# Instance norm in 3D on one core: three 64 KiB slots, each store one load behind, squares on two engines

## The chip, the cores and the metric

The kernel runs on one core of one Trainium2 chip. The metric is the device time of one execution, in microseconds (us); lower is better. The core has a matrix engine (PE), VectorE (DVE), ScalarE (ACT), GpSimd (POOL) and SyncE (SP), which run their own instruction streams and meet at semaphores. Data moves between the device memory (HBM) and the on-chip memory (SBUF, 128 partitions) by transfers that SP issues here; 16 DMA engines carry them out. PSUM is the small memory that PE writes its products to.

## What is computed

```python
# x: (8, 64, 32, 64, 64) float32, eps: 1e-5
mean = np.mean(x, axis=(2, 3, 4), keepdims=True)
var = np.var(x, axis=(2, 3, 4), keepdims=True)
return ((x - mean) / np.sqrt(var + eps)).astype(np.float32)
```

There are 8 x 64 = 512 instances of 32 x 64 x 64 = 131,072 numbers, 512 KiB each. Every number is read once and written once: 268.44 MB in and 268.44 MB out. The variance is taken in a second pass over the data in SBUF, around the mean that the first pass gave.

## The kernel before

**Tiling.** An instance is spread over 16 partitions (`SPLIT`), so a tile holds 8 instances: 128 partitions of 8192 columns, 32 KiB in each partition, 4 MiB in all. There are 64 tiles. The pool has six buffers (`SLOTS`).

**One tile's work** (`compute`, L80). `cut` is half of the columns. DVE sums the first half (L83) while ACT sums the second (L86, an Identity activation whose accumulator is the sum; its written output, `unused`, is thrown away). A matmul with a block matrix of 1/131,072 (L93) adds the sums of an instance's 16 partitions, so that each partition gets the two halves of its instance's mean, and DVE adds them with a minus sign (`neg_mean`, L95). ACT then squares the whole tile with that bias and accumulates (L103). A second matmul gives the variance (L107), ACT takes the square root (L109), DVE the reciprocal (`scale`, L111) and the product `bias` (L113). Then the tile is normalized in place: DVE the second half (L114), ACT the first (L122).

**Order.** Everything stands in the order written (`manual_schedule`). The loop (L130) first loads and computes tile g, then stores tile g - 4 (`LAG`). All loads (L77) and stores (L135) are issued by SP and go through one queue, in order. SP's stream is thus five loads, then a store and a load in turn, and five stores after the last load. A store waits on SP for both engines' last work on its tile. From the seventh on, a load waits on SP until the store that empties its buffer has landed; everything behind it in SP's stream waits too.

The lines that the change and the steps below touch are L77, L83, L86, L93, L95, L103, L107, L114, L122, L135 and the loop at L130.

Of the kernel before, what the change touches and what calls it, by code (L numbers as in the profile page):

```python
# [1 line left out]

# [4 lines left out]


@with_exitstack
def kernel(  # L10
    ctx: ExitStack,
    tc: tile.TileContext,
    x: bass.AP,
    eps: bass.AP,
    out: bass.AP,
):
    nc = tc.nc
    fp32 = mybir.dt.float32
    Alu = mybir.AluOpType
    Act = mybir.ActivationFunctionType  # L20

    P = 128
    B, C, D, H, W = x.shape
    n_inst = B * C
    n_elem = D * H * W
    eps_f = float(eps)

    SPLIT = 16
    IPT = P // SPLIT
    F = n_elem // SPLIT  # L30
    n_tiles = n_inst // IPT
    SLOTS = 6

    x_t = x.rearrange("b c d h w -> (b c) (d h w)").rearrange(
        "(k i) (s f) -> k (i s) f", i=IPT, s=SPLIT
    )
    out_t = out.rearrange("b c d h w -> (b c) (d h w)").rearrange(
        "(k i) (s f) -> k (i s) f", i=IPT, s=SPLIT
    )

    singles = ctx.enter_context(tc.tile_pool(name="singles", bufs=1))
    data_pool = ctx.enter_context(tc.tile_pool(name="data", bufs=SLOTS))
    stat_pool = ctx.enter_context(tc.tile_pool(name="stats", bufs=4))
    psum_pool = ctx.enter_context(
        tc.tile_pool(name="psum", bufs=2, space=bass.MemoryType.PSUM)
    )


    avg = singles.tile([P, P], fp32, name="avg")
    nc.vector.memset(avg, 1.0 / n_elem)  # L50
    nc.gpsimd.affine_select(  # L51
        out=avg,
        in_=avg,
        pattern=[[-SPLIT, IPT], [0, SPLIT]],
        compare_op=Alu.is_ge,
        fill=0.0,
        base=0,
        channel_multiplier=1,
    )
    nc.gpsimd.affine_select(  # L60
        out=avg,
        in_=avg,
        pattern=[[SPLIT, IPT], [0, SPLIT]],
        compare_op=Alu.is_ge,
        fill=0.0,
        base=SPLIT - 1,
        channel_multiplier=-1,
    )

    eps_t = singles.tile([P, 1], fp32, name="eps_t")  # L70
    nc.vector.memset(eps_t, eps_f)  # L71

    unused = singles.tile([P, F], mybir.dt.uint8, name="unused")

    def load(g):
        t = data_pool.tile([P, F], fp32, name="xt")
        nc.sync.dma_start(out=t, in_=x_t[g])  # L77
        return t

    def compute(t):  # L80
        cut = F // 2
        sums = stat_pool.tile([P, 2], fp32, name="sums")
        nc.vector.reduce_sum(  # L83
            out=sums[:, 0:1], in_=t[:, :cut], axis=mybir.AxisListType.X
        )
        nc.scalar.activation(  # L86
            out=unused[:, cut:],
            in_=t[:, cut:],
            func=Act.Identity,
            accum_out=sums[:, 1:2],  # L90
        )
        mean_ps = psum_pool.tile([P, 2], fp32, name="mean_ps")
        nc.tensor.matmul(out=mean_ps, lhsT=avg, rhs=sums, start=True, stop=True)  # L93
        neg_mean = stat_pool.tile([P, 1], fp32, name="neg_mean")
        nc.vector.tensor_reduce(  # L95
            out=neg_mean,
            in_=mean_ps,
            axis=mybir.AxisListType.X,
            op=Alu.add,
            negate=True,  # L100
        )
        squares = stat_pool.tile([P, 1], fp32, name="squares")
        nc.scalar.activation(  # L103
            out=unused, in_=t, func=Act.Square, bias=neg_mean, accum_out=squares
        )
        var_ps = psum_pool.tile([P, 1], fp32, name="var_ps")
        nc.tensor.matmul(out=var_ps, lhsT=avg, rhs=squares, start=True, stop=True)  # L107
        std = stat_pool.tile([P, 1], fp32, name="std")
        nc.scalar.activation(out=std, in_=var_ps, func=Act.Sqrt, bias=eps_t)  # L109
        scale = stat_pool.tile([P, 1], fp32, name="scale")  # L110
        nc.vector.reciprocal(out=scale, in_=std)  # L111
        bias = stat_pool.tile([P, 1], fp32, name="bias")
        nc.vector.tensor_mul(out=bias, in0=neg_mean, in1=scale)  # L113
        nc.vector.tensor_scalar(  # L114
            out=t[:, cut:],
            in0=t[:, cut:],
            scalar1=scale,
            scalar2=bias,
            op0=Alu.mult,
            op1=Alu.add,  # L120
        )
        nc.scalar.activation(  # L122
            out=t[:, :cut], in_=t[:, :cut], func=Act.Identity, scale=scale, bias=bias
        )


    LAG = 4
    tiles = {}
    with tc.manual_schedule():
        for g in range(n_tiles + LAG):  # L130
            if g < n_tiles:
                tiles[g] = load(g)
                compute(tiles[g])
            if g >= LAG:
                nc.sync.dma_start(out=out_t[g - LAG], in_=tiles.pop(g - LAG))  # L135


# [1 line left out]
_INS = ['x', 'eps']  # L139
_OUTS = [((8, 64, 32, 64, 64), 'float32')]  # L140

_NUMBERS = {'eps': 9.999999747378752e-06}


# [26 lines left out]
```

## Time and profile before

| what | value |
|---|---|
| median of 4 runs | 1252.68 us (1250.03 to 1254.28) |
| the profiled execution's own time | 1254.28 us |
| its span (first to last instruction) | 1252.6 us |
| bytes moved | 536.88 MB by queue q1, 429 GB/s over the span |
| ACT busy | 960.1 us, 77% |
| DVE busy | 467.1 us, 37% |
| PE busy | 73.7 us, 6% |
| one load, issue to landing, median | 29.0 us |
| one store, issue to landing, median | 38.3 us |

Busy time is the sum of an engine's instructions. The profile also has the span in 40 slices, with the share of the 16 DMA engines that was busy in each and the GB/s that they moved; a chain, which goes back from the last instruction to whatever released it at each step; groups of equal instructions, with the mean duration in ns and the idle time ahead of them; and a record of each DMA packet with its start, duration and size. The profiled execution is the slowest of the four runs.

### The profile page before, as it was taken

Reading aid. Unit: us, or ns where it says so; the run is one execution under the profiler, and the core shown is the slowest. Engines: PE = TensorE matmul, PEld = TensorE weight load, DVE = VectorE, ACT = ScalarE, POOL = GpSimd, SP = SyncE. Lnnn points to the kernel's source line nnn. Section 1 sums busy time; section 2 is a strip of 40 time slices with the busy share of each in tenths; the row PEclk is TensorE's granted clock in tenths of the full one; section 3 lists DMA queues with packets and bytes.
Section 4 is the critical chain, followed back from the end, with each engine's and each line's share of the span. In section 5 each row is a group of like instructions: output and inputs, shape, how many; then the busy total and the mean of one; then the engine's idle time right before and its main releaser. Section 6 shows DMA issues by size and latency. Waiting matters only on the chain.

```text
span 1252.6 us, 1770 instructions
## 1 busy us (share of the span) xinstructions
PE 73.7 (6%) x256; PEld 64.2 (5%) x256; DVE 467.1 (37%) x322; ACT 960.1 (77%) x386; POOL 0.9 (0%) x6
## 2 busy tenths in 40 slices
PE   0000000000000000000000000000000000000000
PEld 0000000000000000000000000000000000000000
DVE  2344443334343343333433334334343343333430
ACT  5898888877777777778777777877777777777780
POOL 0000000000000000000000000000000000000000
DMA  9999999999999999999999999999999999999998
GB/s 402 419 434 428 431 424 429 429 420 435 435 434 430 430 435 435 430 432 435 432 430 434 435 428 435 435 423 433 433 429 432 431 432 435 434 433 434 434 430 355
DMA packets 18443, 536.99 MB, mean 429 GB/s; under 512 B 2048, under 2 KB 2048, under 8 KB 2048
## 3 DMA queue, kind: packets, MB, share of 16 engines
q1 hardware_dynamic: 18432, 536.88, 99.7%
q14 instruction: 9, 0.07, 0.0%
q8 instruction: 2, 0.03, 0.0%
HBM read 268.44 MB, written 268.44 MB: 429 GB/s over the span
## 4 chain that ended last, share of the span: by engine, by line
DMA 92%; ACT 3%; DVE 1%; SPq 1%; issue 0%; PE 0%; ACTq 0%
DMA out_dram<-xt 89%; DMA xt<-in_x_dram 3%; ACT unused L103 2%; ACT xt L122 1%; SPq L77 1%; DVE sums L83 1%; ACT unused L86 0%; PE mean_ps L93 0%; ACT L109 0%; PE var_ps L107 0%; ACT std L109 0%; DVE scale L111 0%; DVE neg_mean L95 0%; DVE bias L113 0%; SPq L135 0%
## 5 line engine op out<-in xcount | busy, mean ns | idle before, releaser
L103 ACT ACTIVATE unused<-xt,neg_mean 128x8192 uint8<-128x8192 f32 x64 | 455.8, 7121 | 99.5 <-DVE neg_mean L95 99.5
L83 DVE TENSOR_REDUCE sums<-xt 128x1 f32<-128x4096 f32 x64 | 282.8, 4418 | 159.4 <-DMA xt<-in_x_dram 159.4
L86 ACT ACTIVATE unused<-xt 128x4096 uint8<-128x4096 f32 x64 | 231.2, 3613 | 87.7 <-DMA xt<-in_x_dram 87.7
L122 ACT ACTIVATE xt<-xt,bias,scale 128x4096 f32<-128x4096 f32 x64 | 243.2, 3801 | 30.4 <-DVE bias L113 30.4
L111 DVE RECIPROCAL scale<-std 128x1 f32<-128x1 f32 x64 | 10.5, 164 | 531.7 <-ACT std L109 531.7
L114 DVE TENSOR_SCALAR xt<-xt,scale,bias 128x4096 f32<-128x4096 f32 x64 | 154.4, 2413 | 2.6 <-DVE bias L113 0.3
L93 PE MATMUL mean_ps<-sums,avg 128*128 128x2 f32 x128 | 36.1, 352 | 658.1 <-DVE sums L83 542.2
L107 PE MATMUL var_ps<-squares,avg 128*128 128x1 f32 x128 | 37.6, 363 | 484.8 <-ACT unused L103 484.8
L93 PEld LDWEIGHTS mean_ps<-sums,avg 128*128 128x128 f32 x128 | 32.1, 311 | 661.9 <-ACT unused L86 644.4
L107 PEld LDWEIGHTS var_ps<-squares,avg 128*128 128x128 f32 x128 | 32.2, 312 | 490.4 <-ACT unused L103 490.4
L109 ACT ACTIVATE std<-var_ps,eps_t 128x1 f32<-128x1 f32 x64 | 16.7, 261 | 42.7 <-PE var_ps L107 42.7
L95 DVE TENSOR_REDUCE neg_mean<-mean_ps 128x1 f32<-128x2 f32 x64 | 10.2, 159 | 55.9 <-PE mean_ps L93 55.9
L86 ACT ACTIVATION_READ_ACCUMULATOR unused<-xt 128x1 f32 x64 | 11.9, 186 | 0.0
L103 ACT ACTIVATION_READ_ACCUMULATOR unused<-xt,neg_mean 128x1 f32 x64 | 11.9, 186 | 0.0
L113 DVE TENSOR_TENSOR bias<-neg_mean,scale 128x1 f32<-128x1 f32 x64 | 10.2, 159 | 2.2
L86 ACT ACT_TABLE_LOAD x1 | 1.3, 1283 | 0.8 <-PEq L152 0.8
L109 ACT ACT_TABLE_LOAD x1 | 1.3, 1283 | 0.0
L50 DVE MEMSET avg<- 128x128 f32 x1 | 0.2, 165 | 0.9 <-PEq L152 0.9
L51 POOL TENSOR_SCALAR_AFFINE_SELECT avg<-avg 128x128 f32<-128x128 f32 x1 | 0.3, 343 | 0.6 <-DVE eps_t L71 0.6
L60 POOL TENSOR_SCALAR_AFFINE_SELECT avg<-avg 128x128 f32<-128x128 f32 x1 | 0.3, 338 | 0.1
L152 POOL MEMSET const-bfloat16-1.0<- 128x1 bf16 x1 | 0.1, 101 | 0.0
L152 POOL MEMSET const-uint8-127<- 128x1 uint8 x1 | 0.1, 101 | 0.0
(3 smaller groups left out, 0.3 us busy)
## 6 DMA issues: line engine op xcount, KB each, us to landing
xt<-in_x_dram SPq DMA_DIRECT2D x64, 4096.0 KB, 29.0
out_dram<-xt SPq DMA_DIRECT2D x64, 4096.0 KB, 38.3
```

Source lines behind the costliest of these rows:

```text
L77: nc.sync.dma_start(out=t, in_=x_t[g])
L83: nc.vector.reduce_sum(out=sums[:, 0:1], in_=t[:, :cut], axis=mybir.AxisListType.X)
L86: nc.scalar.activation(out=unused[:, cut:], in_=t[:, cut:], func=Act.Identity, accum_out=sums[:, 1:2],)
L93: nc.tensor.matmul(out=mean_ps, lhsT=avg, rhs=sums, start=True, stop=True)
L95: nc.vector.tensor_reduce(out=neg_mean, in_=mean_ps, axis=mybir.AxisListType.X, op=Alu.add, negate=True,)
L103: nc.scalar.activation(out=unused, in_=t, func=Act.Square, bias=neg_mean, accum_out=squares)
L107: nc.tensor.matmul(out=var_ps, lhsT=avg, rhs=squares, start=True, stop=True)
L109: nc.scalar.activation(out=std, in_=var_ps, func=Act.Sqrt, bias=eps_t)
L111: nc.vector.reciprocal(out=scale, in_=std)
L113: nc.vector.tensor_mul(out=bias, in0=neg_mean, in1=scale)
L114: nc.vector.tensor_scalar(out=t[:, cut:], in0=t[:, cut:], scalar1=scale, scalar2=bias, op0=Alu.mult, op1=Alu.add,)
L122: nc.scalar.activation(out=t[:, :cut], in_=t[:, :cut], func=Act.Identity, scale=scale, bias=bias)
```

## The change

**Tiles.** A slot now has 16,384 columns, 64 KiB in each partition and 8 MiB in all. It holds 16 instances, each spread over 8 partitions. There are 31 whole slots, and the last 16 instances are cut into three pieces of 8, 4 and 4 instances (8192, 4096 and 4096 columns), which lie side by side in one slot. The pool has three slots instead of six. Three averaging matrices are built instead of one, for 8, 16 and 32 partitions to an instance; their entries are negative, so that the matmuls give the mean and the variance with a minus sign.

**Order.** SP issues three loads, the stores of slots 0 and 1, and then in turn the load of slot g + 2 and the store of slot g + 1. A load waits for the store of slot g - 1, which had its place. The three loads of the pieces stand ahead of the store of the last whole slot, and the three stores of the pieces at the end.

**Shares.** The sum is split 29/64 to DVE and 35/64 to ACT. The squares, which were ACT's alone, are split: ACT takes 13/16, and DVE takes the first 3/16 (3072 columns) in two instructions: it subtracts the mean in place and then multiplies the result with itself and accumulates, with the product thrown away to PSUM. Two matmuls add the two parts of the variance in PSUM. The normalization is split in three: ACT the last 25/64, DVE the next 27/64 with scale and bias, and DVE the first 3/16, already centred, with the scale alone.

The diff, cut to its core:

```diff
-    SPLIT = 16
-    IPT = P // SPLIT
-    F = n_elem // SPLIT
-    n_tiles = n_inst // IPT
-    SLOTS = 6
+    SLOTS = 3
+    COLS = 16384
+    BIG = P * COLS // n_elem
+    groups = [(i, BIG) for i in range(0, n_inst - BIG, BIG)]
+    n_big = len(groups)
+    tail = [
+        (n_inst - BIG, BIG // 2),
+        (n_inst - BIG // 2, BIG // 4),
+        (n_inst - BIG // 4, BIG // 4),
+    ]
...
+    def averaging(split):
+        neg = singles.tile([P, P], fp32, name=f"neg{split}")
+        nc.vector.memset(neg, -1.0 / n_elem)
...
+    negs = {n: averaging(P // n) for n in sorted({n for _, n in groups + tail})}
+    of_act = singles.tile([P, COLS - COLS * 3 // 16], mybir.dt.uint8, name="of_act")
+    of_dve = psum_one.tile([P, COLS * 3 // 16], fp32, name="of_dve")
+    def rows(ap, first, n):
+        return ap[first : first + n].rearrange("i (s f) -> (i s) f", s=P // n)
+    def load(t, first, n):
+        nc.sync.dma_start(out=t, in_=rows(x_f, first, n))
-    def compute(t):
-        cut = F // 2
+    def compute(t, n):
+        w = t.shape[1]
+        a = w * 29 // 64
+        b = w * 3 // 16
+        c = w * 39 // 64
+        neg = negs[n]
         nc.vector.reduce_sum(
-            out=sums[:, 0:1], in_=t[:, :cut], axis=mybir.AxisListType.X
+            out=sums[:, 0:1], in_=t[:, :a], axis=mybir.AxisListType.X
         )
         nc.scalar.activation(
-            out=unused[:, cut:],
-            in_=t[:, cut:],
+            out=of_act[:, : w - a],
+            in_=t[:, a:],
             func=Act.Identity,
             accum_out=sums[:, 1:2],
         )
...
         nc.scalar.activation(
-            out=unused, in_=t, func=Act.Square, bias=neg_mean, accum_out=squares
+            out=of_act[:, : w - b],
+            in_=t[:, b:],
+            func=Act.Square,
+            bias=neg_mean,
+            accum_out=squares[:, 1:2],
+        )
+        nc.vector.tensor_scalar(
+            out=t[:, :b],
+            in0=t[:, :b],
+            scalar1=neg_mean,
+            scalar2=None,
+            op0=Alu.add,
+        )
+        nc.vector.tensor_tensor_reduce(
+            out=of_dve[:, :b],
+            in0=t[:, :b],
+            in1=t[:, :b],
+            scale=1.0,
+            scalar=0.0,
+            op0=Alu.mult,
+            op1=Alu.add,
+            accum_out=squares[:, 0:1],
         )
-        nc.tensor.matmul(out=var_ps, lhsT=avg, rhs=squares, start=True, stop=True)
+        nc.tensor.matmul(
+            out=neg_var, lhsT=neg, rhs=squares[:, 0:1], start=True, stop=False
+        )
+        nc.tensor.matmul(
+            out=neg_var, lhsT=neg, rhs=squares[:, 1:2], start=False, stop=True
+        )
...
+        nc.scalar.activation(
+            out=t[:, c:], in_=t[:, c:], func=Act.Identity, scale=scale, bias=bias
+        )
         nc.vector.tensor_scalar(
-            out=t[:, cut:],
-            in0=t[:, cut:],
+            out=t[:, b:c],
+            in0=t[:, b:c],
             scalar1=scale,
             scalar2=bias,
             op0=Alu.mult,
             op1=Alu.add,
         )
-        nc.scalar.activation(
-            out=t[:, :cut], in_=t[:, :cut], func=Act.Identity, scale=scale, bias=bias
-        )
+        nc.vector.tensor_scalar(
+            out=t[:, :b], in0=t[:, :b], scalar1=scale, scalar2=None, op0=Alu.mult
+        )
...
     with tc.manual_schedule():
-        for g in range(n_tiles + LAG):
-            if g < n_tiles:
-                tiles[g] = load(g)
-                compute(tiles[g])
-            if g >= LAG:
-                nc.sync.dma_start(out=out_t[g - LAG], in_=tiles.pop(g - LAG))
+        for g in range(SLOTS):
+            load(whole(g), *groups[g])
+        compute(tiles[0], groups[0][1])
+        store(tiles[0], *groups[0])
+        for g in range(1, n_big - 1):
+            compute(tiles[g], groups[g][1])
+            store(tiles[g], *groups[g])
+            if g + 2 < n_big:
+                load(whole(g + 2), *groups[g + 2])
+        last = list(pieces(whole(n_big)))
+        for t, first, n in last:
+            load(t, first, n)
+        g = n_big - 1
+        compute(tiles[g], groups[g][1])
+        store(tiles[g], *groups[g])
+        for t, first, n in last:
+            compute(t, n)
+            store(t, first, n)
```

## The prediction

> **What bounds the kernel now.** I read the 40 slices of the span first, then the DMA queues and the chain.
>
> ```profile
> DMA  9999999999999999999999999999999999999998
> GB/s 402 419 434 428 431 424 429 429 420 435 435 434 430 430 435 435 430 432 435 432 430 434 435 428 435 435 423 433 433 429 432 431 432 435 434 433 434 434 430 355
> ...
> q1 hardware_dynamic: 18432, 536.88, 99.7%
> ...
> DMA 92%; ACT 3%; DVE 1%; SPq 1%; issue 0%; PE 0%; ACTq 0%
> ```
>
> The 16 DMA engines never rest, and the chain is transfers for 92% of the span. The bytes stay the same, so the change can only win what lies above them: 536.88 MB at the best slices' 435 GB/s are 1234.2 us, against a span of 1252.6. Coarser windows (the last two columns are DMA share and GB/s) show where these 18 us are:
>
> ```profile
> 0.00:60.00 60.00, 2.91 (x10) 2.51 (x10) 19.20 (x14) 42.97 (x17) 0.89 (x6) 1.00 0.98 411
> 60.00:300.00 240.00, 16.40 (x56) 14.06 (x56) 101.38 (x70) 204.79 (x85) 0.00 (x0) 1.00 1.00 428
> 300.00:700.00 400.00, 23.50 (x82) 20.58 (x82) 149.67 (x104) 308.35 (x125) 0.00 (x0) 1.00 1.00 433
> 700.00:960.00 260.00, 15.44 (x54) 13.54 (x54) 98.99 (x67) 200.83 (x81) 0.00 (x0) 1.00 1.00 432
> ```
>
> From 60 to 300 us the engines are as busy as later, yet move 428 and not 433 GB/s. The packets' records say why. Of 16,384 data packets (32 KiB, one row of a tile) 15,642 took 1213 ns. A transfer without a slow packet, 8 packets on each engine, takes 9.681 us from its first packet to the next transfer's, load or store. The slow packets, up to 2.3 us, are nearly all the last two of a load with a store behind it: a stall at the switch from reading to writing HBM. In the packets' starts I joined each engine's packets. The slowest engine begins at 1.8, would need 128 x 9.681 = 1239.2 and so end at 1241.0; it ends at 1251.4 (the fastest at 1245.4). So 10.4 us are stalls on the slowest engine, at 60 switches. The rest is 1.2 us to the span's end and 1.7 us around it (1254.28 - 1252.6).
>
> ACT and DVE wait for loads, at 77% and 37%. What the new order asks of them are these groups (count | busy us, mean ns):
>
> ```profile
> L103 ACT ACTIVATE unused<-xt,neg_mean 128x8192 uint8<-128x8192 f32 x64 | 455.8, 7121 | 99.5 <-DVE neg_mean L95 99.5
> L83 DVE TENSOR_REDUCE sums<-xt 128x1 f32<-128x4096 f32 x64 | 282.8, 4418 | 159.4 <-DMA xt<-in_x_dram 159.4
> L86 ACT ACTIVATE unused<-xt 128x4096 uint8<-128x4096 f32 x64 | 231.2, 3613 | 87.7 <-DMA xt<-in_x_dram 87.7
> L122 ACT ACTIVATE xt<-xt,bias,scale 128x4096 f32<-128x4096 f32 x64 | 243.2, 3801 | 30.4 <-DVE bias L113 30.4
> ...
> L114 DVE TENSOR_SCALAR xt<-xt,scale,bias 128x4096 f32<-128x4096 f32 x64 | 154.4, 2413 | 2.6 <-DVE bias L113 0.3
> ```
>
> **One slot's compute.** L86 and L103 give 0.856 ns a column and 105 ns for ACT with a thrown-away output. Sums: DVE 7424 columns at L83's 4418/4096 are 8.0 us; ACT 8960 are 7.8 and 0.2 to read the accumulator. From the sums to the squares the last tile took 1.0 us. Squares: ACT 13,312 columns, 11.5 + 0.2 = 11.7. Beside it DVE subtracts the mean over 3072 columns (L114's rate: 1.8) and multiplies and accumulates, which no row shows. At nothing it changes nothing. At L83's rate it is 3.3; at three times that, as the upper bound for two operands and a PSUM output, 9.9, and 11.7 with the subtraction, just hidden behind ACT. I take 3.3, L83 being the nearest (fp32, one result). From squares to normalizing 1.4 us in the last tile, plus a second matmul pair at 0.3. Normalizing: ACT 6400 columns at L122's rate 5.9; DVE 9984 columns at L114's rate 5.9. Sum: 8.0 + 1.0 + 11.7 + 1.7 + 5.9 = 28.3 us.
>
> **Steady state: the queue.** SP's stream becomes store g, load g+2, and so on. The store of g waits for compute g, and behind it in SP wait load g+2 and all later ones. Compute g starts when load g has landed; until the queue is dry it still holds store g-1 and load g+1, 4 x 9.68 = 38.7 us. Compute (28.3) and a latency of about 1.5 end 9 us earlier, more than the 6 us by which the engines' ends drift apart now. Load g+2 also waits for store g-1, which has landed 19 us before that queue runs dry. So no gap is added: cost 0, hidden behind one store and one load. If the cover went, each us of compute above 37 would cost one us in each of 31 slots.
>
> **Start.** Load 0 lands about 9.7 us after the first tile did now (13.1), at 22.7. Slot 0 takes 28.3 and the 1.3 us table load that the trace shows before the first root; slot 1 ends at 80.6, and the first packet comes 1.0 us after an issue (0.80 to 1.81 now): 81.6. Three loads and store 0 keep the DMA engines until 1.8 to 2.6, + 77.4, + 1.6 of stalls seen in the first loads now, = 80.8 to 81.6. A gap of 0 to 1 us; I take 0.5. Each us more per slot costs 2 us here.
>
> **End.** Behind the last load piece stand store 30 (19.4) and the piece stores (9.7, 4.8, 4.8). Slot 30 is done 10 us before that piece lands, the three pieces (about 15, 8 and 8) some 5, 13 and 21 us after it, when 19.4, 29.1 and 33.9 are due. No gap. The matrices and memsets are done in the 22 us before load 0 lands.
>
> **Fewer transfers.** 128 become 68. Starts inside a transfer are 1195 ns apart on average, over its end 1315, so an end costs at most 120 ns; at least 0, if reading merely runs ahead and bytes set the pace. A transfer at 435 GB/s would be 9.64, so I take 0.04 us: 60 x 0.04 = -2.4 (0 to -7.2). Whether a 64 KiB row goes as one packet or as two doesn't alter the number of ends.
>
> "SBUF — State Buffer", section "The DMA setup-cost knee", of the Trainium skill says that every transfer pays some 2 us whatever its size. By it, as an estimate, 60 fewer save 120 us, and the kernel would go below the time of its bytes. The row of 9.681 us, end to end, shows that a full queue hides this; the measurement decides.
>
> **Fewer switches.** Load-to-store switches fall from 60 to 30 (after loads 2 to 30 and the last piece). The slowest engine's 10.4 us become 5.2. Bounds: 0, as between 300 and 700 us, and more than now in the rival below.
>
> One rule speaks against the larger rows. "DMA: Bandwidth & Descriptors", section "Latency and other measured facts", has copies slowing when the rows of neighbouring partitions lie a large power of two apart in HBM: 207 GB/s a direction at 512 KiB against 214. The distance doubles here from 32 to 64 KiB, for which the page has no figure; were the whole 3% due, it would be an estimated +41 us. The trace's 433 GB/s at 32 KiB shows no loss, and no run shows 64 yet.
>
> **Sum.** 1.8 + 1239.2 - 2.4 + 5.2 + 0.5 + 1.2 + 1.7 = 1247.2, against 1254.28 for the profiled execution: -7.1. That one is 1.6 above the median; if these 1.6 are stalls too, half of them go anyway, and against the median I get 1246.4, rounded to **1246 us**.
>
> **Rivals.**
> *The stalls go with time, not with switches, and ends are free*: 10.4 stays, -2.4 goes, the gap stays: 1252.7 + 0.5 = 1253. For it: they cluster (60 to 300, 700 to 960 us). Against: they sit at the switches. 0.17.
> *The start opens*: if the unseen multiply costs four times L83's rate, 13.2, DVE needs 15.0 against 11.7; two slots add 6.6 at the start: 1253. Against: it needs more than three times the nearest row. 0.05.
> *Slower: longer reads, longer stalls.* Place: each of the 30 switches. After five loads in a row, 20 MiB, with all engines within 0.6 us of each other, the stall was 0.9 us on average; from 60 to 300 us, after 4 MiB each, the distance of load issues was 19.86 against 19.37 later, 0.49 a switch. Linear in the length, 8 MiB give 0.6: 30 x 0.6 = 18 in place of the 4.4 in my median's sum, 1260. It decides from 0.49 a switch kept up to the end. Against: from 300 to 700 us there are almost no stalls, with the engines 3 us apart; for it: every slot of the new start finds them in step. 0.15.
> *No stalls at all and ends at 0.08*: 1246 - 4.4 - 2.4, about 1239 to 1241. 0.08.
>
> **How the numbers follow.** My forecast has 0.55, which makes 1246. A measurement of this kernel can tell some 0.3%, 3.8 us, from no change: 1248.9 to 1256.4 is "same". Faster is 0.55 + 0.08 = 0.63; same 0.17 + 0.05 = 0.22; slower 0.15. The range goes from 1241 (all stalls gone) to 1258, two above the line from which it is slower; it leaves out the deeper ends on both sides.
>
> **What would show it.** Right: DMA slices near 435 with few dips; 68 issues; SP's waits on DVE or ACT short after slot 1; no idle DMA stretch but near 81 us; a last packet near 1244. Wrong: SP waiting for ACT or DVE in each slot (compute above 37 us); the multiply above 10 us; slices of 420 to 428 through the whole span (stalls kept up); packets above 2.43 us for 64 KiB.

## Result: 1.2 us faster, a fifth of the forecast

The changed kernel takes 1250.31 us (median of 41 runs, 1248.82 to 1252.25), the kernel before 1251.51 us (61 runs, 1250.03 to 1254.28): a ratio of 0.999, with a 95% interval of 0.9985 to 0.9994. The sign was forecast and the time lies in the range, but of the forecast 6 us only 1.2 came. That is below the 0.3% which the prediction called "same". The profiled execution took 1250.83 us, with a span of 1249.1.

The page of the changed kernel: share of busy DMA engines and GB/s in 40 slices, the queue, and the chain by engine.

```profile
DMA  9999999999999999999999999999999999999998
GB/s 403 437 437 420 430 426 437 437 422 430 437 428 426 437 437 434 437 434 428 432 432 437 432 433 428 434 437 437 432 437 434 433 437 434 428 432 437 428 433 353
...
q1 hardware_dynamic: 9792, 536.88, 99.6%
...
DMA 46%; ACT 25%; DVE 17%; another core or an unknown queue 8%; PE 2%; issue 1%; SPq 0%; ACTq 0%
```

The DMA engines are as busy as before, with 9792 packets in place of 18432. The chain has changed its look and not its meaning. Each store is now released by DVE or ACT, so the chain runs through the compute, and SP's waits (line and what it waited for: us in total, times, longest us) say the same:

```profile
SPq L184 <- DVE xt L166: 1196.8, 34, 48.6
...
SPq L90 <- DMA out_dram<-xt: 3.4, 1, 3.4
```

Yet a released store lands 30.5 us after its issue (median) though it takes only 19.3 us to move: for 11 us it stands in a queue that still has work. Compute isn't the bound; a chain that shows who released an instruction doesn't show that the queue behind it was full. The windows say where the rate is below 433:

```profile
0.00:60.00 60.00, 2.29 (x8) 2.01 (x8) 28.20 (x16) 35.95 (x11) 2.13 (x10) 1.00 1.00 419
60.00:300.00 240.00, 11.56 (x40) 10.03 (x40) 120.70 (x60) 162.91 (x40) 0.00 (x0) 1.00 1.00 430
300.00:700.00 400.00, 17.34 (x60) 15.06 (x60) 197.33 (x92) 257.56 (x61) 0.00 (x0) 1.00 1.00 433
700.00:960.00 260.00, 12.14 (x42) 10.55 (x42) 128.94 (x61) 170.87 (x41) 0.00 (x0) 1.00 1.00 433
```

The same shape as before, with only 2 GB/s more from 60 to 300 us (430 against 428), where the halved stalls should have shown. The compute came out as priced. The groups of whole slots (shapes kept apart):

```profile
L115 ACT ACTIVATE of_act<-xt,neg_mean 128x13312 uint8<-128x13312 f32 x31 | 353.0, 11388 | 35.0 <-DVE neg_mean L112 35.0
L100 DVE TENSOR_REDUCE sums<-xt 128x1 f32<-128x7424 f32 x31 | 244.4, 7885 | 348.1 <-DMA xt<-in_x_dram 348.1
...
L155 ACT ACTIVATE xt<-xt,bias,scale 128x6400 f32<-128x6400 f32 x31 | 177.4, 5721 | 14.7 <-DVE bias L154 14.7
L158 DVE TENSOR_SCALAR xt<-xt,scale,bias 128x6912 f32<-128x6912 f32 x31 | 120.3, 3879 | 1.1
L129 DVE CUSTOM_DVE_ANT_0 of_dve<-xt 128x3072 f32<-128x3072 f32 x31 | 104.4, 3367 | 1.1
```

The multiply that no row of before showed (L129) costs 3.4 us, and 3.3 was taken. The first slot's sums begin at 22.73 us (22.7 forecast), and from the second slot on a slot takes 27 to 28 us (28.3 forecast).

**How the packet records are read from here on.** Without a stall a packet of 16, 32 or 64 KiB takes 611, 1213 or 2418 ns. What a packet takes above that is its stall; "stalls" below is their sum, averaged over the 16 engines, whose last packets end 5 to 8 us apart in most runs. "Clean" is the time that an engine needs for its share of 8 MiB between 110 and 1140 us, stalls taken off.

### The profile page after: what moved, and what is told of

Its sections match the earlier page's. It is cut to its first block, busy times and chain, and to the rows that moved or that the text cites. A ratio compares the mean times of both kernels' runs of the same rounds, so it can differ in the third digit from the quotient of the medians.

```text
span 1249.1 us, 1213 instructions
## 1 busy us (share of the span) xinstructions
PE 59.0 (5%) x204; PEld 51.2 (4%) x204; DVE 618.1 (49%) x310; ACT 812.0 (65%) x206; POOL 2.1 (0%) x10
## 3 DMA queue, kind: packets, MB, share of 16 engines
q1 hardware_dynamic: 9792, 536.88, 99.6%
## 4 chain that ended last, share of the span: by engine, by line
DMA 46%; ACT 25%; DVE 17%; another core or an unknown queue 8%; PE 2%; issue 1%; SPq 0%; ACTq 0%
DMA xt<-in_x_dram 44%; ACT of_act L115 18%; DVE sums L100 12%; ACT xt L155 6%; DVE xt L158 2%; DMA out_dram<-xt 2%; DVE xt L166 1%; PE halves L110 1%; PE neg_var L143 1%; ACT of_act L103 1%; ACT std L148 0%; DVE scale L152 0%; DVE neg_mean L112 0%; DVE bias L154 0%
## 5 line engine op out<-in xcount | busy, mean ns | idle before, releaser
L103 ACT ACTIVATE of_act<-xt 128x8960 uint8<-128x8960 f32 (+2 forms) x34 | 245.8, 7229 | 344.3 <-DMA xt<-in_x_dram 344.3
L100 DVE TENSOR_REDUCE sums<-xt 128x1 f32<-128x7424 f32 (+2 forms) x34 | 252.6, 7430 | 349.8 <-DMA xt<-in_x_dram 349.8
L115 ACT ACTIVATE of_act<-xt,neg_mean 128x13312 uint8<-128x13312 f32 (+2 forms) x34 | 365.0, 10736 | 37.9 <-DVE neg_mean L112 37.9
L155 ACT ACTIVATE xt<-xt,bias,scale 128x6400 f32<-128x6400 f32 (+2 forms) x34 | 183.9, 5408 | 16.1 <-DVE bias L154 16.1
L158 DVE TENSOR_SCALAR xt<-xt,scale,bias 128x6912 f32<-128x6912 f32 (+2 forms) x34 | 124.7, 3668 | 1.2
L129 DVE CUSTOM_DVE_ANT_0 of_dve<-xt 128x3072 f32<-128x3072 f32 (+2 forms) x34 | 108.1, 3179 | 1.2
L122 DVE TENSOR_SCALAR xt<-xt,neg_mean 128x3072 f32<-128x3072 f32 (+2 forms) x34 | 58.7, 1726 | 1.2
L166 DVE TENSOR_SCALAR xt<-xt,scale 128x3072 f32<-128x3072 f32 (+2 forms) x34 | 58.5, 1720 | 0.0
L143 PE MATMUL neg_var<-squares,neg 128*128 128x1 f32 x68 | 20.0, 363 | 180.9 <-ACT of_act L115 180.9
L140 PE MATMUL neg_var<-squares,neg 128*128 128x1 f32 x68 | 20.0, 363 | 179.6 <-DVE squares L129 179.6
L143 PEld LDWEIGHTS neg_var<-squares,neg 128*128 128x128 f32 x68 | 17.1, 312 | 183.8 <-ACT of_act L115 183.8
L140 PEld LDWEIGHTS neg_var<-squares,neg 128*128 128x128 f32 x68 | 17.1, 312 | 182.6 <-DVE squares L129 182.6
L129 DVE DVE_READ_ACCUMULATOR2_ANT squares<- 128x1 f32 x34 | 4.8, 141 | 0.0
## 6 DMA issues: line engine op xcount, KB each, us to landing
out_dram<-xt SPq DMA_DIRECT2D x31, 30.5
```

What stands on the lines that cost most here:

```text
L100: nc.vector.reduce_sum(out=sums[:, 0:1], in_=t[:, :a], axis=mybir.AxisListType.X)
L103: nc.scalar.activation(out=of_act[:, : w - a], in_=t[:, a:], func=Act.Identity, accum_out=sums[:, 1:2],)
L115: nc.scalar.activation(out=of_act[:, : w - b], in_=t[:, b:], func=Act.Square, bias=neg_mean, accum_out=squares[:, 1:2],)
L122: nc.vector.tensor_scalar(out=t[:, :b], in0=t[:, :b], scalar1=neg_mean, scalar2=None, op0=Alu.add,)
L129: nc.vector.tensor_tensor_reduce(out=of_dve[:, :b], in0=t[:, :b], in1=t[:, :b], scale=1.0, scalar=0.0, op0=Alu.mult, op1=Alu.add, accum_ou ...
L140: nc.tensor.matmul(out=neg_var, lhsT=neg, rhs=squares[:, 0:1], start=True, stop=False)
```

## Experiments

The prediction's theory is that a stall is paid at every switch from load to store, so that 30 switches cost half of 60. The rival formed from the new profile: stalls are paid while the 16 engines come to the switch together, and they themselves drive the engines apart. Then the sum doesn't follow the number of switches. A third: they belong to the first 300 to 500 us of a run, whatever the cause.

The times stand beside those of before from the same chip and hour.

| kernel | switches | median us (runs) | before beside it | clean us for 8 MiB | stalls up to 100 us | stalls later |
|---|---|---|---|---|---|---|
| before, two profiles | 60 | 1251.51 (61) | | 19.370, 19.369 | 1.8, 1.5 | 4.0, 2.0 |
| changed, two profiles | 30 | 1250.31 (41) | 1251.51 | 19.322, 19.322 | 1.7, 1.9 | 3.6, 3.1 |
| e1_pairs | 30 | 1252.38 (11) | 1251.50 | 19.368 | 1.6 | 2.6 |
| e2_halves | 30 | 1254.73 (11) | 1251.50 | 19.367 | 1.9 | 3.1 |
| e3_before_stagger | 60 | 1252.83 (11) | 1251.50 | 19.368 | 1.2 | 0.7 |
| e4_after_stagger | 30 | 1249.83 (11) | 1251.50 | 19.322 | 1.7 | 0.7 |
| e5_rows32 | 30 | 1252.12 (11) | 1251.81 | 19.361 | 1.4 | 2.9 |
| e6_norm_act | 30 | 1271.87 (4) | 1251.81 | | 1.8 | 12.8 |
| e7_whole_tail | 30 | 1258.60 (4) | 1251.81 | | 1.8 | 3.1 |
| e8_bands | 30 | 1252.69 (11) | 1251.81 | 19.323 | 1.8 | 2.8 |
| f1_stagger_half | 30 | 1250.37 (11) | 1252.16 | | 1.2 | 2.4 |
| f2_resync | 29 | 1276.28 (4) | 1252.16 | | 1.6 | 6.1 |

**Half the switches alone (e1).**

```diff
-        for g in range(n_tiles + LAG):
-            if g < n_tiles:
-                tiles[g] = load(g)
-                compute(tiles[g])
-            if g >= LAG:
-                nc.sync.dma_start(out=out_t[g - LAG], in_=tiles.pop(g - LAG))
...
+        for g in range(SLOTS, n_tiles, 2):
+            tiles[g] = load(g)
+            tiles[g + 1] = load(g + 1)
+            store(g - 4)
+            store(g - 3)
+            compute(tiles[g])
+            compute(tiles[g + 1])
```

> The kernel before with loads and stores in pairs: six loads, then two stores, two loads and so on. 128 transfers of 4 MiB as before, 32 KiB packets as before, but 31 load-to-store switches in place of 60. If the stall is paid per switch (the prediction's step), the 7.6 us of stalls in a median run of before (1251.51 less 1.8 + 1239.2 + 1.2 + 1.7) halve and the time is about 1247.7. If stalls are paid until the 16 engines have drifted some 3 us apart, whatever the number of switches, the sum stays within 1.5 us: 1250 to 1253. If they go with time (some outside cause in the first 300 to 500 us), also about 1251.5, but then they end near 300 us, as in before, and not after some 12 switches (near 500 us).

1252.38 us, 1.0008 of before (0.9999 to 1.0016): halving the switches (to 30; the 31 above is one too many) saves nothing. The stalls behind the first 100 us, 2.6 us, lie between those of the two profiles of before. They don't end at 300 us either; they go on past 600. But they don't fit the in-step rival either: at the three switches from 100 to 180 us the engines came within 0.7 to 0.8 us of each other, and the mean stall was only 0.02 to 0.03 us. Most of the 2.6 us came later, with the engines over 3 us apart.

**Twice the transfers, half the packet (e2).**

```diff
     def load(t, first, n):
-        nc.sync.dma_start(out=t, in_=rows(x_f, first, n))
+        r, h = rows(x_f, first, n), t.shape[1] // 2
+        nc.sync.dma_start(out=t[:, :h], in_=r[:, :h])
+        nc.sync.dma_start(out=t[:, h:], in_=r[:, h:])
```

> The changed kernel with each load and store issued as two transfers of half the columns, 32 KiB packets and twice the transfers; switches, slots and compute unchanged. In the changed kernel's records a 64 KiB packet took 2418 ns against 2 x 1213, and a transfer without stalls 19.32 us against 2 x 9.68. If that is the whole of what the larger slot wins, 64 x 0.043 = 2.75 us are lost again: 1250.31 + 2.75 = 1253.1. If ends and packets cost nothing, 1250.3.

The clean time is before's again, 19.367, so 64 x 0.045 = 2.9 us are lost. The median is 4.4 above the changed kernel's; the other 1.5 us, within the reach of the engines' uneven ends, stay unexplained.

**One transfer, small packets (e5).**

```diff
-        return ap[first : first + n].rearrange("i (s f) -> (i s) f", s=P // n)
+        return ap[first : first + n].rearrange(
+            "(j i) (s f) -> (i s) j f", j=2, s=2 * P // n
+        )
```

> The changed kernel with each whole slot still one transfer of 8 MiB, but its partitions made of two rows of 32 KiB that lie 4 MiB apart in HBM, as two tiles of the kernel before would; 68 transfers, 32 KiB packets. A partition then holds pieces of two instances and the statistics mix them, so the numbers aren't the reference's; shapes and work are. If the gain of the larger slot comes with the packet (some 8.5 ns each: 1213 against 2418 / 2), a transfer-equivalent takes 19.37 us as in before, and 64 x 0.048 = 3.1 us are lost: 1253.4. If it comes with the end of a transfer (the prediction's step), nothing is lost: 1250.3. Beside it the layout is told apart: if stalls while the engines are in step are larger in the changed kernel because its rows lie 64 KiB apart, they shrink here from some 0.3 us a switch in the first 300 us to the 0.05 to 0.1 of the kernel with pairs.

Clean 19.361: of the 0.048 us that the larger slot saves on 8 MiB, 0.039 come with the packet (8 fewer on each engine, 4.9 ns each) and 0.009 with the end of a transfer. The median, 1252.12, lies between the two expectations, and before was 0.3 us slower on that chip than beside the changed kernel: the packet records decide here, not the time. At 0.2 to 0.3 us a switch between 100 and 250 us, rows 32 KiB apart stall about as much as rows 64 KiB apart in the changed kernel (0.3 to 0.4 in its first profile, 0.1 to 0.3 in its second); the distance of the rows isn't shown to matter.

**Engines apart from the start (e3, e4).** Six small extra loads give some of the engines more to do before the first store:

```diff
+    STEPS = [(104, 425), (88, 425), (63, 486), (49, 486), (25, 680), (3, 3400)]
+    def stagger(t, src):
+        at = 0
+        for rows, cols in STEPS:
+            nc.sync.dma_start(
+                out=t[:rows, at : at + cols], in_=src[:rows, at : at + cols]
+            )
+            at += cols
...
+        load(tiles[0], *groups[0])
+        stagger(tiles[2], rows(x_f, *groups[2]))
```

> The kernel before with six small extra loads behind the first five loads, over 13, 11, 9, 7, 5 and 3 rows or multiples of them, into a buffer that the sixth load overwrites. They should give the DMA engines 0 to 3 us of extra work in steps of 0.5 us, so that the engines are apart before the first store. If stalls need engines in step, the packet records show few stalls (under 2 us on an engine) and the time is 1251.5 + 3.0 - 6 or so: 1248 to 1250, though one engine has 3 us more to do. If each switch stalls anyway, or an outside cause does it, the 3 us come on top: 1253.5 to 1254.5.

> The same six extra loads in the changed kernel, behind the first load, into the third slot. In-step theory: the 9 us of stalls on the slowest engine fall to 2 or so, 3.0 us of extra work are added: 1250.3 + 3.0 - 7 = 1246.5, within 1245 to 1248. Per-switch or outside cause: 1253 to 1253.5.

The stalls are mostly gone, as the in-step theory said: behind the first 100 us, 0.7 us are left in either kernel, and no run without these six loads has less than 2.0. In e4 the first and the last engine are 3.9 us apart behind the first loads, evenly spread, against 0.6 in the changed kernel. The windows from 100 to 300 us (last column GB/s), first of the kernel before, without and with the extra loads:

```profile
100.00:300.00 200.00, 13.46 (x46) 11.55 (x46) 82.18 (x57) 170.14 (x69) 0.00 (x0) 1.00 1.00 427
```

```profile
100.00:300.00 200.00, 13.43 (x46) 11.52 (x46) 82.26 (x57) 172.11 (x69) 0.00 (x0) 1.00 1.00 433
```

and of the changed kernel with them:

```profile
100.00:300.00 200.00, 8.29 (x29) 7.24 (x30) 95.99 (x45) 125.88 (x29) 0.00 (x0) 1.00 1.00 434
```

ACT and DVE do the same work in the first two. But the second profiles of the two kernels (f3 and f4 below), without extra loads, have this in the same window, before and changed:

```profile
100.00:300.00 200.00, 13.44 (x46) 11.52 (x46) 82.29 (x57) 172.75 (x69) 0.00 (x0) 1.00 1.00 431
```

```profile
100.00:300.00 200.00, 8.65 (x30) 7.51 (x30) 96.83 (x46) 126.84 (x31) 0.00 (x0) 1.00 1.01 435
```

So the rate of one window decides nothing; the sums of the stalls do. The times missed their ranges, too. In e3 some 3.3 us of extra work on the busiest engine outweigh what is saved (+1.3); e4's median is 0.5 below the changed kernel's, where 2.3 to 5.3 were expected. The slowest engine, which alone sets the time, still ended 3.1 us behind the mean in e4 and 4.5 us in e3.

**Gentler or cheaper steps (f1, e8).** f1 halves the columns of `STEPS`. e8 loads nothing twice: it cuts the last columns of the second load into transfers over 120 + 8, 104 + 24 and 88 + 40 partitions.

> The changed kernel with the six extra loads of half the size: 0 to 1.65 us of extra work in steps of some 0.25 us. The extra loads of full size took the stalls behind the first 100 us from 3.6 us an engine to 0.8, at 3.3 us of added work on the busiest engine: 1249.8. In-step theory: with half the steps the engines are apart by 2.2 us at the first store, where the changed kernel still paid 0.2 to 0.3 a switch; some 1.5 us of stalls remain behind 100 us, and the time lies between 1248.5 and 1250. If only the amount of extra work counted, 1250.3 - 0.2.

> The changed kernel with the second load cut so that its last 1920 columns come in three bands of six transfers over 120 + 8, 104 + 24 and 88 + 40 partitions. Nothing is loaded twice, but the engines get unequal shares: by the row counts the lower ones about 0.6 us more than now and the upper ones up to 2.3 us less, so that they are apart before the first store. In-step theory: few stalls after that, as with the extra loads (2.5 us an engine in place of 5.3), without those loads' 3.3 us: 1246.5 to 1248.5. If it is the extra loads themselves, or only engines spread evenly, that help, 1250 to 1251.

f1: 2.4 us of stalls remain where 1.5 were expected. Its time is 0.9987 of before on its chip (0.9979 to 0.9996), which can't be told from the changed kernel's 0.999 or e4's 0.9986. e8 missed: the stalls are hardly fewer, and the time is 1252.69. Its packets, joined engine by engine, say how far it put the engines apart: behind the first three loads the first and the last are 3.0 us apart, but eleven of the 16 still lie within 0.6 us. So e8 spread only a few engines, and it is no test of engines that are all apart. One thing the three runs share: at the first switch, where the changed kernel's engines (0.6 us apart) stalled 1.2 and 1.1 us in its two profiles, those of e4, f1 and e8 (3.9, 1.9 and 3.0 us apart) stalled 0.03 us or less.

**Together again in mid-run (f2).**

```diff
-            if g + 2 < n_big:
+            if g == 17:
+                load(whole(g + 1), *groups[g + 1])
+            if g != 16 and g + 2 < n_big:
                 load(whole(g + 2), *groups[g + 2])
```

> The changed kernel with the load of slot 18 moved behind the store of slot 17. The queue then runs dry twice, near 700 and 770 us: a slot's compute of 27.9 us and 1.2 us to the first packet, against one transfer of 19.3, give 9.8 us each, and the engines start again together. Time 1250.3 + 19.6 = 1270, plus new stalls. In-step theory: after the gaps the load-to-store switches stall again, by 0.2 to 0.4 us each for some five to ten switches, though until 700 us they had come to under 0.1: 2 to 3 us an engine, most of it between 720 and 1000 us. If stalls belong to the first 300 to 500 us of a run, or to something outside, next to none come back.

Windows of this run:

```profile
100.00:680.00 580.00, 24.75 (x86) 21.50 (x86) 286.12 (x132) 370.01 (x88) 0.00 (x0) 1.00 1.00 433
680.00:700.00 20.00, 1.17 (x4) 1.00 (x4) 7.57 (x6) 13.88 (x4) 0.00 (x0) 1.00 0.30 128
...
770.00:1000.00 230.00, 10.38 (x36) 9.01 (x36) 108.77 (x54) 144.93 (x36) 0.00 (x0) 1.00 1.00 428
```

After the gaps (all engines idle for 9.4 and 8.4 us, 14.2 and 9.7 on average) the rate falls from 433 back to 428, late in the run. From 700 to 1000 us 3.7 us of stalls come, against 0.4 in the changed kernel's first profile and 0.7 in its second, so stalls don't belong to the beginning of a run alone. Three switches take 2.5 of it, not five to ten with 0.2 to 0.4 each as was expected: 0.7 each at the end of the first store after either gap, which is a switch to a load, and 1.1 at the next switch to a store. Those to a load stalled otherwise only in e6 (below), where the queue runs nearly dry too. The rest, about 1 us, is little above the changed kernel's. So f2 doesn't tell whether engines brought together or a queue that had just been dry makes the new stalls. With the faster engines' longer idling this makes 1276.3 in place of 1270.

**Both kernels once more (f3, f4)**, for a second profile of each.

> The kernel before once more, for a second profile. Stalls of 5 to 6.5 us an engine, most of them before 300 us, a span of 1248 to 1252; clean transfer 9.685 us.

> The changed kernel once more, for a second profile. Stalls of 4.5 to 6 us an engine, most of them before 500 us, a span of 1247 to 1250; clean transfer 19.32 us.

One execution took 1251.42 us and the other 1251.92. The clean times repeat to 1 ns; the stalls don't. Before had 3.6 us an engine in this execution, less than expected, against 5.9 in the first; the changed kernel had 5.0 against 5.3. So a difference of 1 or 2 us in stalls between two single profiles says nothing, and the drop to 0.7 with the extra loads does.

**The start's cover and the pieces (e6, e7).** e6 gives ACT DVE's share of the normalization; e7 sets `tail = [(n_inst - BIG, BIG)]`.

> The changed kernel with ACT normalizing all of the 13,312 columns behind the first 3072, DVE's share of 6912 gone: ACT takes 11.5 in place of 5.7 us, so a slot's compute goes from 27.9 (measured in its first slots) to 33.6 us. By the prediction's step on the start, 2 us for each us more, less the slack of 1.7 us that the trace shows there: 11.4 - 1.7 = 9.7 us, all of it near 81 us, and nothing in the steady state, whose 38.6 us still cover 33.6 and the latency: 1260. If the steady state were bound by compute in part, more: some us for each of 31 slots. If compute doesn't matter at all, 1250.3.

> The changed kernel with the last slot whole instead of in three pieces. Its compute of 27.9 us begins when the load lands, and behind that load the queue has one store of 19.3 us: the last store's first packet comes about 29.4 us after the landing, a gap of 10 us: 1260. If the pieces bring nothing, 1250.3.

e6's windows at the start, and e7's at the end:

```profile
50.00:75.00 25.00, 1.17 (x4) 1.00 (x4) 9.94 (x5) 24.07 (x4) 0.00 (x0) 1.00 1.01 419
75.00:85.00 10.00, 0.59 (x2) 0.50 (x2) 7.34 (x4) 8.84 (x4) 0.00 (x0) 1.00 0.48 210
85.00:95.00 10.00, 0.00 (x0) 0.00 (x0) 2.50 (x1) 10.00 (x2) 0.00 (x0) 1.00 0.49 210
```

```profile
1210.00:1228.00 18.00, 1.14 (x4) 1.00 (x4) 12.16 (x5) 16.88 (x3) 0.00 (x0) 1.00 0.70 303
1228.00:1237.00 9.00, 0.59 (x2) 0.50 (x2) 5.93 (x4) 7.21 (x4) 0.00 (x0) 1.00 0.00 0
1237.00:1257.00 20.00, 0.00 (x0) 0.00 (x0) 0.00 (x0) 0.00 (x0) 0.00 (x0) 1.00 0.97 419
```

Both gaps are where and as long as expected: all engines idle for 9.0 us at 81.4 in e6 (9.7 expected), for 9.4 us at 1227.8 in e7 (10). e7's time, 1258.6, follows. e6's doesn't: it lost 21.6 us, not 9.7. Besides the gap (9.4 us on average over the engines) it has 9.4 us more of stalls, all through the run, and a gap of 1.5 at the end. With 33.6 us of compute a store is ready some 3.5 us before the queue runs dry (38.6 - 33.6 - 1.5), less than the engines lie apart, so the faster ones meet a nearly empty queue. The packet records point the same way: 6.3 us of the stalls fall on the last two packets of a store with a load behind it, where the changed kernel has 0.1, and apart from the switch after the first gap (0.7) they begin at 578 us, when the engines had come 4.2 us apart. That the thin queue makes them is still an inference; no run took it apart. But engines far apart don't keep stalls away here.

## Why the prediction was wrong, point by point

**Steady state, start and end: right.** No gap is added in the changed kernel. Slot 1's store was issued at 78.49, the first transfers kept the engines until 81.2, and no idle stretch shows there; 0.5 had been taken, 0 came. The two shares that make this possible, e6's and e7's, are worth 10 us each at their place. But the remark that compute could grow to 37 us unpunished was too generous: at 33.6 the stalls rose.

**Fewer transfers: right in size, wrong in cause.** -2.4 was taken; 64 x 0.048 = -3.1 came. Four fifths of it belong to the larger packet, which the prediction gave no price, one fifth to the end of a transfer (e5). The prediction's bound of 120 ns for an end rests on starts 1195 and 1315 ns apart, and the records don't bear these out: joined engine by engine, packets without a stall start 1210 ns apart inside a transfer of before and 1215 ns apart over its end. That -2.4 came close is luck.

**Larger rows: no harm.** The section "Latency and other measured facts" of "DMA: Bandwidth & Descriptors" in the Trainium skill has no figure for rows 64 KiB apart. Here the clean rate rose, from 433.1 to 434.1 GB/s (8 MiB on 16 engines in 19.370 and 19.322 us).

**Fewer switches: the step that failed**, "The slowest engine's 10.4 us become 5.2". What is left on the slowest engine of a median run when start, clean transfers and end are taken off is 1251.51 - 1.8 - 1239.7 - 2.9 = 7.1 us in before and 1250.31 - 1.8 - 1236.6 - 2.9 = 9.0 us in the changed kernel. Forecast was a loss of half; what came is 1.9 more. So of the 3.1 us from packets and ends 1.2 remain, which is the result.

What stands in place of the step: the place of the stalls was right, mostly the last packets of a load with a store behind it (4.8 of the 5.9 us in the first profile of before). Wrong was that their sum follows the number of switches. Over the whole run it is 5.9 and 3.6 us an engine with 60 switches in before, 4.2 with 30 in e1, and 5.3 and 5.0 with 30 in the changed kernel. From the packet records, mean stall at a switch, and number of switches, by how far apart the first and the last engine end the load:

| engines apart | before | before again | changed (whole slots) | changed again | e1 |
|---|---|---|---|---|---|
| under 1 us | 0.50 (2) | 0.37 (2) | 0.62 (3) | 0.39 (4) | 0.24 (4) |
| 1 to 3 us | 0.18 (5) | 0.09 (7) | 0.31 (5) | 0.16 (3) | 0.06 (4) |
| over 3 us | 0.06 (53) | 0.03 (51) | 0.06 (21) | 0.09 (22) | 0.07 (22) |

The switches that the change took away were mostly the cheap ones of the last row. Up to 3 us apart, there are 7 and 9 in before and 8 and 7 in the changed kernel, and they cost 1.9 and 1.4 us in all against 3.4 and 2.1. But the last row isn't free: it makes up 3.1 and 1.3 us in before and 1.2 and 2.0 in the changed kernel.

Shown is that halving the switches doesn't halve the stalls (e1: 4.2 us of them, and a time 4.7 us above the 1247.7 that halving would give), and that loads which spread the engines before the first store take most of them away (e3, e4). That a stall needs engines close together isn't shown: three close switches of e1 hardly stalled, and e6 stalled with its engines over 4 us apart.

The prediction's own remark that from 300 to 700 us "there are almost no stalls, with the engines 3 us apart" spoke against every switch costing the same; it was held against the slower rival and not against the step itself. (First to last they were 5.4 to 6.8 us apart there.) The slower rival, "longer reads, longer stalls", had the higher price of close switches on its side, but e1, whose reads between two stores are as long, paid no such price, and the stalls weren't kept up to the end. The rival that let stalls go with time gave 1253 and came nearest, for another reason.

Also missed: the prediction halved the slowest engine's time as if all engines stalled alike. The mean stall is 5.9 and 3.6 us in the two profiles of before, 5.3 and 5.0 in those of the changed kernel; the slowest engine ends 3 to 5 us behind the mean in each. In the runs of the other edits it was 2.5 to 4.6 us, except in e6 and e7, where a gap near the end lets all engines finish together. Why a stall arises, and what makes one engine the last, stays open; the records don't name the engine.

## What to carry to other kernels

When a single queue keeps all DMA engines busy, count what is left above the bytes by packet and by place before promising any of it: larger packets gave their 3 us of clean time in every profile, while stalls that fall unevenly on their occasions aren't halved by halving these. Larger slots take away cover at both ends, so the first stores and the last slot need work of their own (10 us each here), and a queue whose margin is smaller than the distance between its engines seems to stall (e6; an inference). A mean over 16 engines isn't the end: the slowest one is.

## What the runs showed of the hardware that was not expected

- A row of 64 KiB goes as one packet. In a full queue a packet costs 4.9 ns and the end of a transfer 9 ns beside the bytes: 19.370, 19.361 and 19.322 us for 8 MiB with 16 packets and 2 ends, 16 and 1, 8 and 1.
- A switch from load to store cost up to 1.2 us an engine on average (the changed kernel's first, engines 0.6 us apart), and 0.03 to 0.09 beyond 3 us apart. Switches from store to load cost 0.1 us in all in a full queue (29 of the changed kernel), but 0.7 each right after the gaps of f2, and 6.3 us in all in e6, whose queue ran nearly dry.
- Six extra loads, some 3.3 us of useless work on the busiest engine, gave the lowest median here: 1249.83 us, 0.9986 of before (0.9978 to 0.9995), against 0.999 (0.9985 to 0.9994) for the changed kernel; the intervals overlap.
